# A two-layer flow-matching trunk: the delta rule's block inverse works in place, small products go round four tiles, some loads move forward

## The chip, the cores and the metric

The kernel runs on one core of one Trainium2 chip. Its metric is the device time of one launch in microseconds (us), as the median of several runs. A core has the engines TensorE (PE, its weight loads listed apart as PEld), VectorE (DVE), ScalarE (ACT) and GpSimd (POOL), and SyncE (SP), which here only issues transfers.

## The reference

Two layers of a hybrid trunk for 1024 latent tokens and 128 context tokens, nine tiles of 128 tokens with 1024 channels each. Cut to what matters here:

```python
mod = jax.nn.silu(cond) @ w_mod + b_mod          # 1024 x 3072: shift, scale, gate
h = _rmsnorm(x, g_pre) * (1 + scale) + shift
z = h @ w_in                                     # columns for branches A, B, C
# A: windowed attention with rotary positions   B: gated MLP over 128-token chunks
# C: bidirectional gated DeltaNet, in chunks of 64 tokens:
a_mat = jnp.where(strict, jnp.einsum('bnihd,bnjhd->bnhij', kb, k) * decay, 0.0)
t_mat = lax.linalg.triangular_solve(a_mat + eye, jnp.broadcast_to(eye, a_mat.shape),
                                    left_side=True, lower=True, unit_diagonal=True)
# ... u, w from t_mat; then a scan over the chunks with a 64 x 64 state per head
x = x + gate * _rmsnorm(concat(A, B, C) @ w_out, g_post)
```

The inverse of I + A for each 64 x 64 strictly triangular A is what the title's substitution computes.

## The kernel before

All eight rows of weights are split into a high and a low float16 part, and a projection of one token tile takes 24 matmuls (`proj_tok`, L170). A planner puts the instructions of each engine in an order when the program is built, by a simulated timeline; on the chip each engine then runs its list in that order and waits where data isn't there.

A layer runs two generators side by side (`merge`, L1124). The chain is branch C: gates (`c_gates`, L355), convolution features (`c_features`, L296, matmuls at L312), and `scan` (L419). The fill is `both` (L1187): the MLP, C's gate, attention (`fill`, L1175, called heavy there), and two column groups of the MLP's gate (`b_gate`, L823). Each yields a cost, and `merge` takes fill worth 0.9 of what the chain yields. `b_gate(k)` starts when the chain has put an entry into the list `light`; until then heavy goes on.

In `scan`, head group 0 is prepared, its inverse solved (`lat_solve`, L661) and its 18 scan steps run (`steps`, L549; matmuls L566 to L597, VectorE's copy `vn` at L585), while head group 1 is prepared; then head group 1 is solved and stepped. The context blocks are solved once beside the first preparation. So a layer has three solves, of which two (latent) have 16 blocks per row and one (context) has 4.

A solve is: `diagonals` (L479) gathers the 32 x 32 diagonal blocks, transposes them into a tile M (L497), clears a tile Y (L499) and sets its diagonal to one (L500). `solve` (L503) does the substitution on VectorE, for m from 31 down to 1, with two instructions (L510 multiplies a column of M by a row of Y, L512 subtracts the product from Y). `inverses` (L516) transposes Y two ways (L520), and multiplies for the off-diagonal block: a first run of matmuls of 32 x 32 by 32 x 32 (L527), a copy by ScalarE (L530), negated copies of the diagonal blocks by ScalarE (L537) and GpSimd (L539), a second run (L543). In both runs the outer loop goes over the four (direction, half) sides, which have different rows and columns of the array, and the inner one over the L blocks:

```python
for (r, half, p1, p2) in sides:
    for j in range(L):
        T.matmul(ps[p2:p2 + 32, 32 * j:32 * j + 32], W[p1:p1 + 32, r, j, ...], ...)
```

Each float32 matmul stands in the trace as two PE instructions, so a latent run is 128 of them and a context run 32.

Between the heads of layer 0's attention, `mod` (L210) forms the modulation vectors of layer 1 and the gate of layer 0 from w_mod: a transfer of 512 KB (L245, two blocks of 128 rows, 512 columns, in one of the two staging buffers `st`), then two matmuls per transfer into 32 columns of the array each (L249), round four places j in turn.

Staged weights go through `load_w` (L148): a transfer on ScalarE's queue, ScalarE's high part (L160), VectorE's low part (L161). All other transfers, the transposing ones of attention too (L953, P to PT), go through SP's queue in its order. `out_layer` (L1044) starts per token tile when branch outputs lie in DRAM (`mix_d`); it loads them (OTm, L1054, two buffers) and multiplies by w_out (L1072).

Of the kernel before, what the change touches and what calls it, by code (L numbers as in the profile page):

```python
# [11 lines left out]
F32 = mybir.dt.float32  # L12
# [28 lines left out]
LT = 9  # L41
AHEAD = 6
FILL = 0.9


@with_exitstack
def hybrid_trunk(
# [64 lines left out]
    V.tensor_copy(idb, ident)  # L112
    CK = per.tile([128, 640], F32, name="CK")
    triI = [CK[:, 0:128], CK[:, 128:256]]
    triL = [CK[:, 256:384], CK[:, 384:512]]
    bdones = CK[:, 512:640]
    selc = per.tile([128, 2], F32, name="selc")
# [5 lines left out]
    def masks():  # L123
        dma(CK, cst[:, 0:640])
        ctmp = stg.tile([128, 256], F32, tag="st", name="ctmp")
        dma(ctmp, cst[:, 640:896])
        G.tensor_copy(triIc16, ctmp[:, 0:128].rearrange("p (r c) -> p r c", r=2))
        G.tensor_copy(mneg, ctmp[:, 128:256].rearrange("p (r c) -> p r c", r=2))
        G.tensor_copy(triL16, CK[:, 256:512].rearrange("p (r c) -> p r c", r=2))

# [79 lines left out]
    def mod(l, vt, mp_, csp, AB, wmp=None):  # L210
# [25 lines left out]
        for part in (1, 0, 2):  # L236
            for cb in (2 * part, 2 * part + 1):
                ps = psp()
                for k2 in range(4):
                    if wmp is not None and part < 2:  # L240
                        st = wmp.tile([128, 4, 256], F32, tag="wm", name=nm("wm"), bufs=16)
                    else:
                        st = stg.tile([128, 4, 256], F32, tag="st", name=nm("st"))
                    s = st.rearrange("p a b -> p (a b)").rearrange("p (k c) -> p k c", k=2)
                    dma(s, w_mod[l, 256 * k2:256 * k2 + 256, 512 * cb:512 * cb + 512].rearrange("(k p) c -> p k c", p=128))  # L245
                    for kk in range(2):
                        k = 2 * k2 + kk
                        j = k % 4
                        T.matmul(ps[32 * j:32 * j + 32, :], csp[:, k, :], s[:, kk, :], start=(k < 4), stop=(k >= 4))  # L249
# [105 lines left out]
    def c_gates(l, cp, gp, out):  # L355
        GB = cp.tile([128, 2, 2, 9, 4], F32, name=nm("GB"))
        wab = gp.tile([128, 8, 2, 16], F16, name="wab")
        sab = gp.tile([128, 8, 16], F32, name="sab")
# [60 lines left out]
    def scan(l, cqk, cv_, gates, oacc, ng, NAc, keep, wo, light):  # L419
# [59 lines left out]
        def diagonals(ep, W, L):  # L479
            D = ep[:, 0:64 * L].rearrange("p (n c) -> p n c", c=32)  # L480
            for r in range(2):
                for half in range(2):
                    for a in range(2):
                        rb = 64 * half + 32 * a
                        src = W[rb:rb + 32, r, :, 32 * a:32 * a + 32]
                        dst = D[rb:rb + 32, L * r:L * r + L, :]
                        if half == r:
                            S_.copy(dst, src)
                        else:
                            V.transpose(dst, src)  # L490
            M = ep[:, 1024:2048]
            Dt = D.transpose([0, 2, 1])
            Mt = M.rearrange("p (r c) -> p c r", c=32)
            if L < 16:
                Dt = bc(Dt, 2, 16 // L)
                Mt = Mt.rearrange("p c (x y) -> p c x y", y=2 * L)
# [6 lines left out]
        def solve(ep, M, Y):  # L503
            m3 = M.rearrange("p (r c) -> p r c", c=32)
            y3 = Y.rearrange("p (r c) -> p r c", c=32)
            for m in range(31, 0, -1):
                tmp = ep[:, 3072:3328]
                w = 32 - m
                t3 = tmp[:, 0:m * w].rearrange("p (r c) -> p r c", c=w)
                V.tensor_tensor(t3, m3[:, 0:m, m:m + 1].to_broadcast([128, m, w]),  # L510
                                y3[:, m:m + 1, m:32].to_broadcast([128, m, w]), op=ALU.mult)
                V.tensor_tensor(y3[:, 0:m, m:32], y3[:, 0:m, m:32], t3, op=ALU.subtract)  # L512
                yield 1.0


        def inverses(ep, W, L, Y):  # L516
# [13 lines left out]
            S_.activation(C_[:, 0:32 * L], ps[:, 0:32 * L], AF.Copy, scale=-1.0)  # L530
            for r in range(2):
                for a4 in range(4):
# [8 lines left out]
            for (r, half, p1, p2) in sides:  # L541
                for j in range(L):
                    T.matmul(ps[p1:p1 + 32, 32 * j:32 * j + 32], C_[p2:p2 + 32, 32 * j:32 * j + 32],  # L543
# [117 lines left out]
        def lat_solve(hg, sv):  # L661
            M, Y = diagonals(sv, Ws[hg], 16)
            yield 4.0
            for i, cost in enumerate(solve(sv, M, Y)):
# [7 lines left out]
        with pool(f"gx{l}", 1) as cx, pool(f"gp{l}0", 2) as gp:  # L672
# [3 lines left out]
            for i, _ in enumerate(preps(gp, todo)):  # L676
                if i == 3:
                    M, Y = diagonals(cx, Wc, 4)
                    ctx_solve = solve(cx, M, Y)
                for _ in range(4):  # L680
# [142 lines left out]
    def b_gate(l, bp, k):  # L823

        cs = slice(128 * k, 128 * k + 128)
        w = bp.tile([128, 8, 2, 256], F16, name=nm("wb"), bufs=1)
        load_w((w_in[l, :, C_BU + 128 * k:C_BU + 128 * k + 128], w_in[l, :, C_BG + 128 * k:C_BG + 128 * k + 128]), 256, w)
        sc = IWS * IWS * IWS * 0.5

        def out(ts, th):  # L830
# [46 lines left out]
    def attention(l, other=iter(())):  # L877
        with pool(f"t3{l}", 1, "right") as p1:
# [25 lines left out]
            def prep(p2, kv, t, wq, wa):  # L904
                pq = psp()
                proj_tok(pq[:, 0:256], t, wq)
                proj_tok(pq[:, 256:512], t, wa)
                rt = p2.tile([128, 128], F32, tag="rt", name=nm("rt"))
                dma(rt, rope[t])
                qa = rope_tile(p2, pq[:, 0:256], 4, rt)  # L910
# [93 lines left out]
            for kv in range(2):  # L1004
                with pool(f"t3b{l}{kv}", 2, "right") as p2:
                    if kv == 0:
# [7 lines left out]
                        for t in ordert:  # L1014
                            ps = psp()
                            proj_tok(ps[:, 0:256], t, wkv)
                            rt = p2.tile([128, 128], F32, tag="rt", name=nm("rt"))
                            dma(rt, rope[t])
                            ka = rope_tile(p2, ps[:, 0:128], 2, rt)
# [23 lines left out]

    def out_layer(l, wo, nextAB):  # L1044
# [99 lines left out]
    for l in range(NL):  # L1144
# [14 lines left out]
        cqk = [q.tile([128, 9, 2, 128], F32, name=nm("cqk")) for q in (c0, cp)]  # L1159
        cv_ = [q.tile([128, 9, 128], F32, name=nm("cv")) for q in (c0, cp)]  # L1160
# [26 lines left out]
        def both():  # L1187
            heavy, k = fill(), 0
            while True:
# [5 lines left out]
                elif k < 2:  # L1195
                    with pool(f"bg{l}{k}", 2, "right") as bp:
                        yield from b_gate(l, bp, k)
                    k += 1
# [76 lines left out]
```

## Time and profile before

| what | value |
|---|---|
| median of 3 runs | 1471.59 us (1468.35 to 1475.64) |
| the profiled execution's own time | 1462.98 us |
| its span, first to last instruction | 1460.2 us |
| mean granted TensorE clock | 0.946 |
| PE busy | 1307.0 us (90%) |
| DVE busy | 941.5 us (64%) |
| ACT busy, POOL busy | 616.9 us, 613.4 us (42% each) |

The span is one execution as the hardware profiler saw it; 2.8 us of the execution's time lie outside it. Busy time is a union of the engine's instructions. A matmul's recorded length has a tail that overlaps the next one's start.

### The profile page before, as it was taken

To read this page: it belongs to the slowest core of one execution; us is meant where nothing else is said; L and a number is where in the kernel's file an instruction comes from. 1 tells how busy PE (TensorE), PEld (TensorE's weight loads), DVE (VectorE), ACT (ScalarE), POOL (GpSimd) and SP (SyncE) were. 2 spreads that over 40 slices of the span, in tenths; PEclk is the share of its full clock that TensorE was granted. 3 is DMA by queue.
4 is the path that set the end of the run, shared out by engine and by line. 5 is a ranking of instruction groups with operands and counts; after the bars stand their busy time and mean duration, and the time that the engine had idled before them with its cause. 6 is when DMAs were issued, how large, how long until landed. Compare 5 with 4: busy or idle time off the path is not lost.

```text
span 1460.2 us, 38255 instructions
## 1 busy us (share of the span) xinstructions
PE 1307.0 (90%) x15479; PEld 1009.7 (69%) x15479; DVE 941.5 (64%) x2230; ACT 616.9 (42%) x1411; POOL 613.4 (42%) x818
## 2 busy tenths in 40 slices
PE   6899989899998699959897999999898769987997
PEld 2665567666667587748786655678787658865886
DVE  2865689987646666753446587687875485767333
ACT  2733454434646116732333444332566313665211
POOL 0761245435556135742132432631668403666200
PEclk8999999999999898969998999999999988998999
DMA  9331044839865117673332122242276311877552
GB/s 358 120 80 55 24 113 106 180 105 222 162 171 87 39 32 144 120 221 76 120 131 84 32 63 68 73 95 64 55 142 120 60 49 40 157 115 166 130 181 103
DMA packets 301562, 162.92 MB, mean 112 GB/s; under 512 B 212622, under 2 KB 277938, under 8 KB 301386
## 3 DMA queue, kind: packets, MB, share of 16 engines
q1 hardware_dynamic: 264301, 127.94, 37.4%
q10 hardware_dynamic: 37085, 32.55, 7.6%
q8 instruction: 121, 1.98, 0.6%
q14 instruction: 55, 0.45, 0.1%
HBM read 95.78 MB, written 24.28 MB: 82 GB/s over the span
## 4 chain that ended last, share of the span: by engine, by line
PE 54%; DVE 14%; DMA 13%; issue 7%; POOL 6%; ACT 4%; SPq 1%; ACTq 0%; DVEq 0%; POOLq 0%
PE ps L170 16%; PE ps L1072 12%; PE ps L312 6%; DMA PT<-P 4%; DMA st<-in_w_in_dram 2%; DMA st<-in_w_mod_dram 2%; PE ps L967 2%; POOL P L951 2%; PE ps L249 2%; DVE y L319 1%; DVE sv L512 1%; PE ps L543 1%; PE ps L527 1%; DVE sv L510 1%; DVE wg L161 1%
## 5 line engine op out<-in xcount | busy, mean ns | idle before, releaser
L170 PEld LDWEIGHTS <-X 128*128 128x128 f16 x3888 | 349.6, 100 | 101.2 <-issue 39.3
L170 PE MATMUL ps<-wg,X 128*128 128x256 f16 x2592 | 328.6, 280 | 10.5 <-DVE wg L161 3.9
L951 POOL TENSOR_TENSOR P<-sS,P 128x512 f16<-128x512 f32 (+2 forms) x144 | 150.9, 1053 | 100.9 <-ACT sS L949 100.2
L1072 PEld LDWEIGHTS <-OTm 128*128 128x128 f16 x1728 | 169.1, 99 | 30.5 <-DMA OTm<-mix_d 8.8
L1072 PE MATMUL ps<-wo,OTm 128*128 128x256 f16 x1296 | 152.1, 276 | 7.6 <-DMA OTm<-mix_d 7.6
L312 PE MATMUL ps<-X,wg 128*128 128x512 f16 (+1 forms) x864 | 146.1, 329 | 1.8 <-ACT wg L160 1.4
L946 DVE CUSTOM_DVE_ANT_0 sS<-ps,am,nsk 128x512 f32<-128x512 f32 (+2 forms) x144 | 95.1, 669 | 49.1 <-POOL P L951 24.6
L948 ACT ACTIVATE P<-sS,nmx 128x512 f16<-128x512 f32 (+2 forms) x144 | 94.0, 660 | 73.0 <-DVE nmx L946 67.4
L312 PEld LDWEIGHTS <-wg 128*128 128x128 f16 x864 | 74.0, 99 | 69.1 <-ACT wg L160 1.8
L170 PE MATMUL ps<-wb,X 128*128 128x256 f16 x864 | 102.5, 279 | 14.4 <-ACT wb L160 12.5
L949 ACT ACTIVATE sS<-sS,nmx 128x512 f32<-128x512 f32 (+2 forms) x144 | 95.1, 660 | 4.2 <-DVE OTA L1001 0.4
L145 POOL TENSOR_TENSOR rs<-ms,mhalf 128x1 f32<-128x1 f32 x36 | 20.7, 576 | 171.9 <-DVE ms L1081 103.7
L967 PE MATMUL ps<-Vt,PT 128*128 128x128 f16 (+1 forms) x992 | 67.9, 211 | 22.8 <-DMA PT<-P 21.8
L319 DVE SCALAR_TENSOR_TENSOR y<-zT,cw,y 128x1156 f32<-128x1156 f32 x48 | 68.9, 1439 | 27.4 <-ACT y L317 26.8
L512 DVE TENSOR_TENSOR sv<-sv 128x31 f32<-128x31 f32 (+15 forms) x186 | 78.4, 421 | 4.1
L967 PEld LDWEIGHTS <-PT 128*128 128x128 f16 x992 | 51.1, 100 | 41.6 <-DMA PT<-P 29.7
L510 DVE TENSOR_TENSOR sv<-sv 128x31 f32<-128x31 f32 (+15 forms) x186 | 74.8, 402 | 4.0
L942 PE MATMUL ps<-KT,qT 128*128 128x128 f16 (+2 forms) x272 | 68.6, 269 | 0.0
L288 DVE TENSOR_SCALAR hf<-ps,AB 128x128 f32<-128x128 f32 x117 | 39.7, 402 | 39.3 <-PE ps L281 39.0
L1075 ACT ACTIVATE sq<-ps 128x512 f32<-128x512 f32 x36 | 21.3, 594 | 99.8 <-PE ps L1072 56.8
L941 PE MATMUL ps<-KT,qT 128*128 128x128 f16 (+2 forms) x272 | 60.3, 271 | 3.6 <-DVE nmx L946 1.8
L161 DVE SCALAR_TENSOR_TENSOR wg<-st,wg 128x1024 f16<-128x1024 f32 x44 | 56.0, 1280 | 10.6 <-ACT wg L160 10.4
(265 smaller groups left out, 2723.8 us busy)
## 6 DMA issues: line engine op xcount, KB each, us to landing
st<-in_w_in_dram ACTq DMA_DIRECT2D x38, 512.0 KB
st<-in_w_mod_dram SPq DMA_DIRECT2D x32, 512.0 KB
OTm<-mix_d SPq DMA_DIRECT2D x18, 512.0 KB
wm<-in_w_mod_dram SPq DMA_DIRECT2D x16, 512.0 KB
xt<-in_x_sample_dram SPq DMA_DIRECT2D x16, 512.0 KB
st<-in_w_out_dram ACTq DMA_DIRECT2D x16, 512.0 KB
mix_d<-OTA SPq DMA_DIRECT2D x36, 128.0 KB
xs<-xt SPq DMA_DIRECT2D x9, 512.0 KB
```

The source lines that it names most:

```text
L161: V.scalar_tensor_tensor(dst[:, 4 * h:4 * h + 4, 1, :cols], s, WS, hi, op0=ALU.mult, op1=ALU.subtract)
L170: T.matmul(ps, X[:, t, k, a, :], wg[:, k, b, c0:c0 + n], start=(i == 0), stop=(i == 23))
L312: T.matmul(ps[:, 0:n], wg[:, k, b, 128 * hg:128 * hg + 128], X[:, t0:t1, k, a, :], start=(i == 0), stop=(i == 23))
L319: V.scalar_tensor_tensor(y, zT[:, tap:tap + 1156], cw[:, tap * 6 + ct:tap * 6 + ct + 1], y, op0=ALU.mult, op1=ALU.add)
L510: V.tensor_tensor(t3, m3[:, 0:m, m:m + 1].to_broadcast([128, m, w]), y3[:, m:m + 1, m:32].to_broadcast([128, m, w]), op=ALU.mult)
L512: V.tensor_tensor(y3[:, 0:m, m:32], y3[:, 0:m, m:32], t3, op=ALU.subtract)
L946: V.tensor_tensor_reduce(sS[:, 0:nk], ps[:, 0:nk], mk, -0.125, nsk[:, hh:hh + 1], ALU.add, ALU.min, accum_out=nmx[:, h:h + 1])
L948: S_.activation(P16[:, 0:nk], sS[:, 0:nk], AF.Exp, bias=nmx[:, h:h + 1], scale=-1.0)
L949: S_.activation(sS[:, 0:nk], sS[:, 0:nk], AF.Exp, bias=nmx[:, h:h + 1], scale=-1.0, accum_out=sm[:, h:h + 1])
L951: G.tensor_tensor(P16[:, nk:2 * nk], sS[:, 0:nk], P16[:, 0:nk], op=ALU.subtract)
L967: T.matmul(pops[:, 128 * h:128 * h + n], PT[:, a * nb + j, :], Vt[:, blist[j], kv].rearrange("p s d -> p (s d)")[:, 0:n], start=(i == 0), ...
L1072: T.matmul(ps[:, 256 * i:256 * i + 256], OTm[:, k, a, :], w[:, k, b, :], start=(n == 0), stop=(n == 23))
```

## The change

Cut to its core:

```diff
-            M = ep[:, 1024:2048]
+            Y = ep[:, 2048:3072]
...
-            V.transpose(Mt, Dt)
-            Y = ep[:, 2048:3072]
-            V.memset(Y, 0.0)
-            V.memset(Y[:, 0:1024:33], 1.0)
-            return M, Y
+            V.transpose(Yt, Dt)
+            V.memset(Y[:, 0:1024:33], -1.0)
+            return Y
...
-            for m in range(31, 0, -1):
+            for m in range(30, 0, -1):
...
-                w = 32 - m
+                w = 31 - m
-                V.tensor_tensor(t3, m3[:, 0:m, m:m + 1].to_broadcast([128, m, w]),
-                                y3[:, m:m + 1, m:32].to_broadcast([128, m, w]), op=ALU.mult)
-                V.tensor_tensor(y3[:, 0:m, m:32], y3[:, 0:m, m:32], t3, op=ALU.subtract)
-                yield 1.0
+                V.tensor_tensor(t3, y3[:, 0:m, m:m + 1].to_broadcast([128, m, w]),
+                                y3[:, m:m + 1, m + 1:32].to_broadcast([128, m, w]), op=ALU.mult)
+                V.tensor_tensor(y3[:, 0:m, m + 1:32], y3[:, 0:m, m + 1:32], t3, op=ALU.subtract)
+                yield 31 / 30
...   in inverses, both runs:
-            for (r, half, p1, p2) in sides:
-                for j in range(L):
+            for j in range(L):
+                for (r, half, p1, p2) in sides:
...   and its copies lose their factor of -1:
-                        S_.activation(dst, src, AF.Copy, scale=-1.0)
+                        S_.copy(dst, src)
-                        G.tensor_scalar(dst, src, -1.0, None, op0=ALU.mult)
+                        G.tensor_copy(dst, src)
...   in mod, for the transfers through the staging buffers:
+                    ch, kq = k2 // 2, k2 % 2
+                    c0 = 512 * cb + 256 * ch
+                    dma(st, w_mod[l, 512 * kq:512 * kq + 512, c0:c0 + 256].rearrange("(k p) c -> p k c", p=128))
+                    for j in range(4):
+                        T.matmul(ps[32 * j:32 * j + 32, 256 * ch:256 * ch + 256], csp[:, 4 * kq + j, :], st[:, j, :],
+                                 start=(kq == 0), stop=(kq == 1))
...   in lat_solve: the entry in light for head group 1 right after diagonals
+            if hg:
+                light.append(hg)
             yield 4.0
...
-                if i == (2 if hg else LT):
+                if not hg and i == LT:
...   in both, EARLY = (8.0, 1.0); b_gate yields 0.0 once, right after its load_w
+                        gate = b_gate(l, bp, k)
+                        yield next(gate)
+                        n = 0.0
+                        while n < EARLY[k]:
+                            got = next(heavy, None)
+                            if got is None:
+                                break
+                            n += got
+                            yield got
+                        yield from gate
...   in b_gate one transfer per pair of tiles:
-            for j, t in enumerate(ts):
-                dma(mix_d[t, :, 4 + k].rearrange("p s c -> p (s c)"), ot[:, j].rearrange("p s c -> p (s c)"))
+            dma(mix_d[ts[0]:ts[0] + n, :, 4 + k].rearrange("t p s c -> p t (s c)"), ot[:, 0:n].rearrange("p t s c -> p t (s c)"))
...   in attention the rotary table once per layer, in place of a tile (rt) per use:
+            rts = p1.tile([128, 9, 128], F32, name="rts")
+            dma(rts, rope.rearrange("t p c -> p t c"))
...   the masks CK are loaded in c_gates once per layer, as its first transfer:
+        CK = gp.tile([128, 640], F32, name="CK")
+        dma(CK, cst[:, 0:640])
...   out_layer's two OTm buffers are halves of one tile in the pool of cqk[0]:
+            OT2 = c0.tile([128, 2, 8, 2, 128], F16, tag="cq0", name=nm("OT2"))
-                OTm = p1.tile([128, 8, 2, 128], F16, tag="OTm", name=nm("OTm"), bufs=2)
+                OTm = OT2[:, ti % 2]
...
+        out_layer(l, wo, c0, nxt[1])
         rs.close()
-        out_layer(l, wo, nxt[1])
```

M and Y become one tile: the substitution overwrites the transposed blocks, with -1 on the diagonal, and yields the negated inverse.

## Rows read from the trace of the kernel before

**Rows 1.** Busy time by stage: engine busy (instructions), PE clock, DMA share, GB/s.

```profile
373.00:500.00 127.00, 111.36 (x1816) 86.89 (x1817) 75.65 (x209) 62.08 (x162) 68.00 (x105) 0.97 0.54 116
500.00:550.00 50.00, 45.10 (x547) 38.92 (x547) 34.58 (x88) 11.02 (x22) 13.44 (x19) 0.84 0.20 54
550.00:653.00 103.00, 82.89 (x1276) 67.21 (x1274) 69.44 (x175) 59.52 (x142) 61.96 (x86) 0.86 0.73 162
```

**Rows 2.** Chain that ended last, in time: start us, us, what.

```profile
360.24 3.86 PE ps L527 x128
...
534.62 3.86 PE ps L527 x128
538.48 4.61 PE ps L170 x26
...
650.02 3.55 DMA OTm<-mix_d
```

**Rows 3.** Timeline, the small products: start us, us, engine, line, count [idle before].

```profile
294.80 0.89 PE L527 MATMUL ps<-sv,NAc 32*32 32x32 f32 x32
...
360.17 3.93 PE L527 MATMUL ps<-sv,NA 32*32 32x32 f32 x128
...
599.79 0.45 PE L566 MATMUL ps<-ident,qk 64*64 64x64 f32 x8
...
1049.49 5.47 PE L527 MATMUL ps<-sv,NA 32*32 32x32 f32 x128 [1.33 <-DVE sv L520]
```

**Rows 4.** Line L539 on POOL: duration ns min/median/max, first and last start.

```profile
L539 POOL TENSOR_SCALAR NA<-sv x16: 1477/1481/1484, 355.7 to 1218.1; 32x512 f32<-32x512 f32 x16
```

**Rows 5.** Timeline of PE, the modulation's matmuls.

```profile
240.65 1.06 PE L249 MATMUL ps<-st,csp 128*32 128x512 f32 x8
...
246.56 1.05 PE L249 MATMUL ps<-st,csp 128*32 128x512 f32 x4
...
408.01 1.05 PE L249 MATMUL ps<-st,csp 128*32 128x512 f32 x4 [1.86 <-DMA st<-in_w_mod_dram]
```

**Rows 6.** Groups by line: busy us, mean ns | idle before and what ended it.

```profile
L249 PE MATMUL ps<-st,csp 128*32 128x512 f32 x128 | 31.4, 619 | 8.8 <-DMA st<-in_w_mod_dram 8.8
L566 PE MATMUL ps<-ident,qk 64*64 64x64 f32 x576 | 36.3, 238 | 4.2 <-ACT qw L572 1.3 <-DVE NA L463 1.3 <-DVE of L751 0.9
L512 DVE TENSOR_TENSOR sv<-sv 128x31 f32<-128x31 f32 (+15 forms) x186 | 78.4, 421 | 4.1
L499 DVE MEMSET sv<- 128x1024 f32 x6 | 5.5, 912 | 1.4 <-DVE sv L490 1.1 <-issue 0.2 <-DVE xc L802 0.2
L869 DVE TENSOR_TENSOR ra<-ps,rt 128x256 f32<-128x256 f32 (+1 forms) x54 | 20.1, 372 | 34.9 <-PE ps L170 22.8 <-DMA rt<-in_rope_dram 5.5 <-DMA out_dram<-ra 1.8
```

**Rows 7.** Timeline around head group 1's solve in layer 0, and its counterpart in layer 1.

```profile
496.00 0.91 DVE L499 MEMSET sv<- 128x1024 f32 x1 [0.28 <-DVE sv L490]
496.83 0.23 DVE L585 COPY vn<-ps 128x128 f32<-128x128 f32 x1
...
497.20 0.69 PE L593 MATMUL ps<-vn,kd 64*64 64x64 f32 x8 [3.27 <-DVE vn L585]
...
500.39 1.38 SPq L647 DMA_DIRECT2D out_dram<-S  x2
503.33 2.00 ACT L160 ACTIVATE wb<-st 128x1024 f16<-128x1024 f32 x2 [8.51 <-DVE sv L512]
504.44 0.80 PE L170 MATMUL ps<-wb,X 128*128 128x256 f16 x3 [5.66 <-ACT wb L160]
...
1184.92 2.00 ACT L160 ACTIVATE wb<-st 128x1024 f16<-128x1024 f32 x2 [8.58 <-DMA out_dram<-S]
```

**Rows 8.** Timeline at the start of layer 1.

```profile
771.15 0.38 SPq L359 DMA_DIRECT2D sab<-in_w_in_dram  x1
...
787.52 2.06 PE L170 MATMUL ps<-wab,X 128*128 128x16 f16 x70
...
790.71 2.13 POOL L291 TENSOR_TENSOR X<-hf,X 128x1024 f16<-128x1024 f32 x1 [0.41 <-ACT X L290]
```

More of the change, by code (lines that the diff above doesn't have):

```diff
@@ L42 @@
 AHEAD = 6
+EARLY = (8.0, 1.0)
 FILL = 0.9
@@ L112, in hybrid_trunk @@
     V.tensor_copy(idb, ident)
[L113 to L116, printed above, removed]
     selc = per.tile([128, 2], F32, name="selc")
@@ L123, in masks @@
     def masks():
-        dma(CK, cst[:, 0:640])
-        ctmp = stg.tile([128, 256], F32, tag="st", name="ctmp")
-        dma(ctmp, cst[:, 640:896])
+        ctmp = stg.tile([128, 512], F32, tag="st", name="ctmp")
+        dma(ctmp[:, 0:256], cst[:, 640:896])
+        dma(ctmp[:, 256:512], cst[:, 256:512])
         G.tensor_copy(triIc16, ctmp[:, 0:128].rearrange("p (r c) -> p r c", r=2))
         G.tensor_copy(mneg, ctmp[:, 128:256].rearrange("p (r c) -> p r c", r=2))
-        G.tensor_copy(triL16, CK[:, 256:512].rearrange("p (r c) -> p r c", r=2))
+        G.tensor_copy(triL16, ctmp[:, 256:512].rearrange("p (r c) -> p r c", r=2))
     mhalf = per.tile([128, 18], F32, name="mhalf")
@@ L241, in mod @@
                         st = wmp.tile([128, 4, 256], F32, tag="wm", name=nm("wm"), bufs=16)
[L242 to L249, printed above, removed]
+                        s = st.rearrange("p a b -> p (a b)").rearrange("p (k c) -> p k c", k=2)
+                        dma(s, w_mod[l, 256 * k2:256 * k2 + 256, 512 * cb:512 * cb + 512].rearrange("(k p) c -> p k c", p=128))
+                        for kk in range(2):
+                            k = 2 * k2 + kk
+                            j = k % 4
+                            T.matmul(ps[32 * j:32 * j + 32, :], csp[:, k, :], s[:, kk, :], start=(k < 4), stop=(k >= 4))
+                        continue
+                    ch, kq = k2 // 2, k2 % 2
+                    c0 = 512 * cb + 256 * ch
+                    st = stg.tile([128, 4, 256], F32, tag="st", name=nm("st"))
+                    dma(st, w_mod[l, 512 * kq:512 * kq + 512, c0:c0 + 256].rearrange("(k p) c -> p k c", p=128))
+                    for j in range(4):
+                        T.matmul(ps[32 * j:32 * j + 32, 256 * ch:256 * ch + 256], csp[:, 4 * kq + j, :], st[:, j, :],
+                                 start=(kq == 0), stop=(kq == 1))
                 mp = mp_.tile([128, 512], F32, tag="mp", name=nm("mp"), bufs=2 if PIPE else 1)
@@ L356, in c_gates @@
         GB = cp.tile([128, 2, 2, 9, 4], F32, name=nm("GB"))
+        CK = gp.tile([128, 640], F32, name="CK")
+        dma(CK, cst[:, 0:640])
+        triI = [CK[:, 0:128], CK[:, 128:256]]
+        triL = [CK[:, 256:384], CK[:, 384:512]]
+        bdones = CK[:, 512:640]
         wab = gp.tile([128, 8, 2, 16], F16, name="wab")
@@ L529, in inverses @@
             C_ = ep[:, 3328:3840]
-            S_.activation(C_[:, 0:32 * L], ps[:, 0:32 * L], AF.Copy, scale=-1.0)
+            S_.copy(C_[:, 0:32 * L], ps[:, 0:32 * L])
             for r in range(2):
@@ L536, in inverses @@
                     if a4 % 2:
-                        S_.activation(dst, src, AF.Copy, scale=-1.0)
+                        S_.copy(dst, src)
                     else:
-                        G.tensor_scalar(dst, src, -1.0, None, op0=ALU.mult)
+                        G.tensor_copy(dst, src)
             ps = psw()
-            for (r, half, p1, p2) in sides:
-                for j in range(L):
+            for j in range(L):
+                for (r, half, p1, p2) in sides:
                     T.matmul(ps[p1:p1 + 32, 32 * j:32 * j + 32], C_[p2:p2 + 32, 32 * j:32 * j + 32],
@@ L661, in lat_solve @@
         def lat_solve(hg, sv):
-            M, Y = diagonals(sv, Ws[hg], 16)
+            Y = diagonals(sv, Ws[hg], 16)
+            if hg:
+                light.append(hg)
             yield 4.0
-            for i, cost in enumerate(solve(sv, M, Y)):
-                if i == (2 if hg else LT):
+            for i, cost in enumerate(solve(sv, Y)):
+                if not hg and i == LT:
                     light.append(hg)
@@ L677, in scan @@
                 if i == 3:
-                    M, Y = diagonals(cx, Wc, 4)
-                    ctx_solve = solve(cx, M, Y)
+                    Y = diagonals(cx, Wc, 4)
+                    ctx_solve = solve(cx, Y)
                 for _ in range(4):
@@ L827, in b_gate @@
         load_w((w_in[l, :, C_BU + 128 * k:C_BU + 128 * k + 128], w_in[l, :, C_BG + 128 * k:C_BG + 128 * k + 128]), 256, w)
+        yield 0.0
         sc = IWS * IWS * IWS * 0.5
@@ L907, in prep @@
                 proj_tok(pq[:, 256:512], t, wa)
-                rt = p2.tile([128, 128], F32, tag="rt", name=nm("rt"))
-                dma(rt, rope[t])
+                rt = rts[:, t, :]
                 qa = rope_tile(p2, pq[:, 0:256], 4, rt)
@@ L1016, in attention @@
                             proj_tok(ps[:, 0:256], t, wkv)
-                            rt = p2.tile([128, 128], F32, tag="rt", name=nm("rt"))
-                            dma(rt, rope[t])
+                            rt = rts[:, t, :]
                             ka = rope_tile(p2, ps[:, 0:128], 2, rt)
@@ L1042, in attention, with out_layer @@
                     finish(p2, *prev.pop())
-    def out_layer(l, wo, nextAB):
+    def out_layer(l, wo, c0, nextAB):
         last = l == NL - 1
@@ L1158, in hybrid_trunk @@
         c0 = rs.enter_context(pool(f"c0{l}", 1, "right"))
-        cqk = [q.tile([128, 9, 2, 128], F32, name=nm("cqk")) for q in (c0, cp)]
+        cqk = [q.tile([128, 9, 2, 128], F32, tag=f"cq{i}", name=nm("cqk")) for i, q in enumerate((c0, cp))]
         cv_ = [q.tile([128, 9, 128], F32, name=nm("cv")) for q in (c0, cp)]
```

8 lines of the change are left out of this document (3 added, 5 removed).

## The prediction, made before the result was known

> **What bounds the kernel now.** I read the page first: PE is busy 90% of the span, DVE 64%. An average hides stages, so the table of stretches came next [rows 1]. In the 127 us of layer 0's first scan PE works 111.4 us and every other engine under 76; in the solve of head group 1 (500 to 550) PE has 45.1 of 50 at a granted clock of 0.84; in the second scan (550 to 653) PE has 82.9 of 103, with DMA at 0.73, the highest share of the three. So a microsecond taken from PE's list counts nearly whole in the first two and perhaps half in the third. The chain of waits then says what stands on the path: among its pieces are all eight runs of small products of the latent solves, as whole blocks of 3.9 us and more, of which two stand in the rows [rows 2]. Last I read the timeline around those blocks, the modulation's matmuls, the two solves of head group 1 and the layer boundary [rows 3 to 8].
>
> **The small products of the inverse.** A latent run is 128 instructions in 3.93 us [rows 3]. An instruction's own recorded length is longer than the distance to the next one's start (0.24 us for L566 [rows 6]); with some 0.2 us for the last one's, one starts every 29 ns. Consecutive ones use the same rows and columns of the array, and none can start before the last has streamed. With the loops exchanged, four neighbours use four different row groups and four different column groups. Does the array overlap them? Two rows bear on it. Eight matmuls of twice the columns that alternate between two corners of the array take 0.45 us [rows 3], 0.21 without the last one's own length [rows 6], where eight starts on one place at twice 29 ns would take 0.46. And eight modulation matmuls on four column groups take 1.06 us where four on two groups take 1.05 [rows 5]: four places cost what two cost. I take full overlap of four: 32 rounds of 29 ns and that length, about 1.2 us, so 2.7 us less per latent run. There are two runs in each of four latent solves: 8 x 2.7 = 21.6 us. A context run of 32 takes 0.89 us [rows 3] and becomes 0.45; four of them give 1.8. One latent run goes at half clock (5.47 us [rows 3]) and would give more; I leave that out. Sum: -23.5 us, bounds 0 (no overlap) and -25.
>
> The Trainium skill, "TensorEngine Tiling (Array Packing)", section "Restrictions and Gotchas", says that different row tiles cannot access the same PSUM bank at once; here all four write one bank, and by that rule the term would be 0. The 0.45 us row has two row tiles in one bank too and speaks against it, for two places; no row has four.
>
> What can eat this gain: between the two runs GpSimd copies four blocks, 1.48 us each [rows 4], 6 us after the first transpose. In layer 0's second solve PE fills the gap with 4.61 us of projection [rows 2]; with the first run 2.7 us shorter, filler still covers the copies' end. If the planner puts the filler elsewhere, the copies set the second run and the first run's gain is lost (below). The copies as such I cost at nothing: the same elements, by a copy in place of a multiply.
>
> **The modulation's loads.** 32 transfers feed 128 instructions. In the timeline they stand as 29 groups: 26 of four (first and last shown) and three of eight, where two transfers had both landed [rows 5]. A group of four is two passes one behind the other, 1.05 us; one instruction is recorded at 0.62 [rows 6], so a pass is 0.43. With half the columns and four places, each transfer's eight instructions are two passes of 0.22, and 0.43 us less per group that stood alone: 26 x 0.43 = 11.2 us of PE. The groups of eight gain nothing. But PE already waited 8.8 us for these transfers [rows 6], once 1.86 at 408 [rows 5], and where the landing decides, a faster matmul waits longer. A transfer's rows shrink from 2 KB to 1 KB, as w_in's have them; I see no cost in that. I take -8, bounds -2 (nothing but the time between a matmul and the next issue) and -11.
>
> **The substitution.** L512 takes 78.4 us over six solves [rows 6], and L510, its partner of the same sizes and count, I put at as much: 26 us a solve. The new one has 30 pairs for 31 and 4960 elements a pair-sum for 5456: between 0.8 (by count) and 2.4 us (by elements) less; I take 1.5. The clear of Y goes, 0.91 us a time [rows 6]. That is 14 us of DVE over six solves. Most of it is covered: beside context and first latent solve PE is full of attention, and in head group 1's solve, projections of the gate run about as long as the substitution. On the path I count the clear where it stood ahead of the scan's copy `vn`, while PE waited 3.27 us for it [rows 7]: 0.9 in each layer; and 1 us per layer for the shorter solve of head group 1, whose end the first run awaits. Sum: -4, bounds 0 and -14.
>
> **The gate's weights and the fill around them.** In both layers ScalarE stands 8.5 us before it converts the gate's weights, and PE stands 5.66 us behind it in layer 0 [rows 7]. The wait is not for the weights: the row of layer 1 names the store of the final state, and in layer 0 that store is issued 2.9 us before the conversion starts [rows 7]: `wb` lies in memory that the scan's tiles held. The earlier load does not move that store. The heads put between load and gate (at least 1.0 of cost, two heads) can start their scores in the hole, but their exponentials are in ScalarE's list around the same blocked conversion: -1 us per layer. The entry in `light` one yield of 4.0 and two steps earlier puts some units of heavy behind gate 1 instead of ahead of it; they move from one PE-full stretch to another and I cost them at nothing. If they left more of the first scan without fill (PE is idle 15.6 of its 127 us already [rows 1]), each unit would cost about its microsecond, up to 5 per layer. Sum: -2, bounds +10 and -11 (both holes closed).
>
> **The transfers.** 54 loads of `rt` become two of 576 KB. DVE waited 5.5 us for them [rows 6]; they also leave SP's queue, in which the transposes of P stand, as do 16 stores of the gate's outputs. First use of the table needs all of it landed, hidden behind the key projections' weights. I take -2, bounds 0 and -6. The masks' 320 KB now go ahead of `sab` in SP's queue in layer 1, whose first conversion waits from 771.15 to 773.46 for that load [rows 8]: one issue of 0.38 us and a share of the bandwidth, +1, bounds +0.4 and +2.5. OTm's new place changes no wait that I can see: the first OTm transfer follows the store it depends on in the chain and takes 3.55 us [rows 2], wherever it lands. `out_layer`'s other pools sit 5.6 KB deeper, over attention's tiles; their loads have some 25 us until use. Costed at 0, 2 at most.
>
> **The sum.** -23.5 - 8 - 4 - 2 - 2 + 1 = -38.5 us against the profiled execution's 1462.98: 1424.5. The median of the runs shown is 8.6 above that execution; the same distance gives 1433, 2.6% less. What a measurement of this kernel can tell from no change is about 0.5%, 7.4 us (1464.2 to 1479.0).
>
> **Rivals.**
> First, half comes back: GpSimd's copies set the second run (2.7 us lost in each of four latent solves, 10.8), and the landing of the modulation's transfers takes the 6 us between -8 and -2. -22, so 1450. For it: the copies' 6 us against 1.2 + filler [rows 2, 4] and the 1.86 us wait [rows 5]. Against: filler stood in all four gaps.
> Second, the small products stay serial, because four rows of tiles into one bank are not four columns into one: the change then doesn't do what its first part says. -38.5 + 23.5 = -15, so 1457. For it: no row shows four row groups. Against: the 0.45 us row [rows 3].
> The rule of "TensorEngine Tiling (Array Packing)" above is this rival.
> Third, slower: OTm's two buffers are now halves of one tile. If waits go by the tile and not by the half, each load waits for the matmuls of the tile before, and each of 16 later tiles pays a load of 3.55 us [rows 2]: +57, with the rest +18, so 1490. It decides from 2.4 us a tile on. Against it: X is one tile as well, and PE reads parts of it at 787.52 while GpSimd writes another part at 790.71 [rows 8].
>
> **How the numbers follow.** The forecast's case, gains mostly whole, 0.63, by its own bounds 1418 to 1446; the first rival 0.22, the second 0.09, the third 0.06. The range is 1412 to 1460: from the forecast with closed holes or full modulation gain, up to the second rival with a few microseconds on it; outside are the third rival, a quarter of the second and the edges of the first two cases, under 2 in 10. Faster by over 0.5% is the first case, the first rival and nearly all of the second: 0.92. Within: 0.03. Slower: the third rival, 0.05.
>
> **What would show it.** Right: L527 and L543 stand as runs of 128 in 1.1 to 1.4 us; each L249 group of eight in 0.6 us; L499 is gone, L510 and L512 have 180 instructions each; ScalarE still waits for the state's store before `wb`; OTm loads run ahead of their tile. Wrong: small products at 3.9 us a run (second rival); a gap on PE just before L543 that GpSimd ends (first); gaps of over 2 us before each tile's L1072 (third). The prediction also fails if the planner's order, made anew for every instruction, opens holes in the scans that none of the steps above names.

## The result and the profile after

The changed kernel takes 1436.9 us (median of 4 runs, 1431.5 to 1439.2), the kernel before 1473.6 us beside it: ratio 0.9723 (95% interval 0.9688 to 0.9757). In later runs of both it was 0.9757 (0.9722 to 0.9792), 1437.3 against 1476.6 us. The mean of the two ratios is 0.974, some 38 us less. 1433 was forecast, so the size is right; the terms behind it are so only in part.

The profiled execution of the changed kernel took 1439.21 us, with a span of 1436.3 us. First its stages, cut where those of [rows 1] now lie (columns as there):

```profile
361.00:488.00 127.00, 111.57 (x1852) 88.50 (x1849) 68.44 (x193) 60.08 (x158) 65.69 (x103) 0.97 0.56 117
488.00:536.00 48.00, 39.90 (x572) 33.48 (x572) 37.39 (x90) 11.54 (x21) 9.15 (x17) 0.86 0.17 50
536.00:634.00 98.00, 80.34 (x1262) 65.29 (x1262) 67.51 (x179) 59.07 (x147) 62.99 (x85) 0.92 0.73 156
```

The first scan looks as before; in the solve PE works 39.9 us where it worked 45.1, and in the second scan the clock is 0.92 where it was 0.86. Now the small products, which answer to [rows 3], from the timeline of PE (first run L532, second run L548):

```profile
296.00 0.45 PE L532 MATMUL ps<-sv,NAc 32*32 32x32 f32 x32
345.30 1.42 PE L532 MATMUL ps<-sv,NA 32*32 32x32 f32 x128
350.58 0.24 PE L548 MATMUL ps<-NA,sv 32*32 32x32 f32 x2
355.43 0.24 PE L548 MATMUL ps<-NA,sv 32*32 32x32 f32 x2
357.80 1.40 PE L548 MATMUL ps<-NA,sv 32*32 32x32 f32 x124
...
1021.65 1.93 PE L532 MATMUL ps<-sv,NA 32*32 32x32 f32 x128 [3.57 <-DVE sv L525]
...
1201.46 1.29 PE L548 MATMUL ps<-NA,sv 32*32 32x32 f32 x128
```

128 instructions stand in 1.3 to 1.4 us where they took 3.93, and 32 in 0.45 where they took 0.89. The first run at 1021.65 took 1.93 us, behind an idle time of 3.57; 1.2 GHz was granted there (the mean clock is 0.82 from 1022 to 1047, below). The second run of the solve that starts at 345 is split: PE starts two instructions at 350.58, two at 355.43, and between them does filler (other work that was ready). Groups by line, as [rows 6] and [rows 4] (busy us, mean ns | idle before and what ended it):

```profile
L251 PE MATMUL ps<-st,csp 128*32 128x256 f32 x256 | 24.1, 390 | 10.3 <-DMA st<-in_w_mod_dram 10.0
L548 PE MATMUL ps<-NA,sv 32*32 32x32 f32 x512 | 6.9, 194 | 0.0
L532 PE MATMUL ps<-sv,NA 32*32 32x32 f32 x512 | 6.3, 204 | 3.6 <-DVE sv L525 3.6
L517 DVE TENSOR_TENSOR sv<-sv 128x30 f32<-128x30 f32 (+9 forms) x180 | 70.5, 392 | 4.4
L876 DVE TENSOR_TENSOR ra<-ps,rts 128x256 f32<-128x256 f32 (+1 forms) x54 | 20.1, 373 | 25.6 <-PE ps L167 16.7 <-POOL ql L925 3.6 <-DMA rts<-in_rope_dram 2.6
L544 POOL COPY NA<-sv 32x512 f32<-32x512 f32 x16 | 9.7, 604 | 11.7 <-DVE sv L525 11.2
L1080 PE MATMUL ps<-wo,OT 128*128 128x256 f16 x1296 | 150.9, 275 | 3.3 <-DMA OT<-mix_d 3.3
```

And the hole at the gate of [rows 7], from the timeline:

```profile
489.25 0.69 PE L598 MATMUL ps<-vn,kd 64*64 64x64 f32 x8 [2.36 <-DVE vn L590]
...
492.40 1.38 SPq L652 DMA_DIRECT2D out_dram<-S  x2
495.26 2.00 ACT L157 ACTIVATE wb<-st 128x1024 f16<-128x1024 f32 x2 [7.39 <-DVE sv L517]
496.37 0.80 PE L167 MATMUL ps<-wb,X 128*128 128x256 f16 x3 [5.54 <-ACT wb L157]
```

It is as wide as before: 5.54 us against 5.66, and the conversion starts 2.9 us after the state's store, as before.

**Where the time went.** A second execution of each kernel was profiled (below). PE's busy time was split in the trace by the level that its clock was granted. As an estimate, a microsecond at 1.2 GHz is counted as half a microsecond of work at 2.4 GHz, so "work at 2.4 GHz" is busy time less half of that part.

| us | before | before, again | after | after, again |
|---|---|---|---|---|
| execution | 1462.98 | 1476.41 | 1439.21 | 1434.24 |
| PE busy | 1307.0 | 1311.3 | 1272.2 | 1272.1 |
| of it at 1.2 GHz | 115.4 | 122.0 | 99.9 | 98.3 |
| work at 2.4 GHz | 1249.3 | 1250.3 | 1222.3 | 1222.9 |
| PE idle in the span | 153.2 | 163.3 | 164.1 | 160.2 |

Between the means of the two pairs the profiled time falls by 33.0 us: 27.2 less work, 9.8 less time lost at the lower clock, 3.9 more idle. Between two executions of a kernel the work repeats within 1 us, the other two within some 10; between kernels with the same matmuls in another order the work too differs, by up to 7 us (1220.9 in `e12_best`, 1228.0 in `e11_poolmul`). The first profile of the kernel before was a quick one: 11 us under the median of its runs above.

### The profile page after: what moved, and what is told of

Read it like the earlier page. It is cut to its first block, busy times and chain, and to the rows that moved or that the text cites. A ratio compares the mean times of both kernels' runs of the same rounds, so it can differ in the third digit from the quotient of the medians.

```text
span 1436.3 us, 38355 instructions
## 1 busy us (share of the span) xinstructions
PE 1272.2 (89%) x15607; PEld 985.7 (69%) x15607; DVE 922.8 (64%) x2212; ACT 613.0 (43%) x1411; POOL 591.1 (41%) x818
## 5 line engine op out<-in xcount | busy, mean ns | idle before, releaser
L167 PE MATMUL ps<-wg,X 128*128 128x256 f16 x2592 | 324.1, 277 | 17.7 <-ACT wg L157 4.5
L1080 PEld LDWEIGHTS <-OT 128*128 128x128 f16 x1728 | 169.6, 99 | 25.2 <-DMA OT<-mix_d 3.7
L1080 PE MATMUL ps<-wo,OT 128*128 128x256 f16 x1296 | 150.9, 275 | 3.3 <-DMA OT<-mix_d 3.3
L975 PEld LDWEIGHTS <-PT 128*128 128x128 f16 x992 | 49.6, 99 | 45.1 <-DMA PT<-P 35.4
L517 DVE TENSOR_TENSOR sv<-sv 128x30 f32<-128x30 f32 (+9 forms) x180 | 70.5, 392 | 4.4
L515 DVE TENSOR_TENSOR sv<-sv 128x30 f32<-128x30 f32 (+9 forms) x180 | 68.9, 383 | 3.9
L157 ACT ACTIVATE wg<-st 128x1024 f16<-128x1024 f32 x44 | 45.3, 1054 | 44.8 <-DMA st<-in_w_in_dram 28.0
```

Of the source, the lines that this page charges most:

```text
L167: T.matmul(ps, X[:, t, k, a, :], wg[:, k, b, c0:c0 + n], start=(i == 0), stop=(i == 23))
L515: V.tensor_tensor(t3, y3[:, 0:m, m:m + 1].to_broadcast([128, m, w]), y3[:, m:m + 1, m + 1:32].to_broadcast([128, m, w]), op=ALU.mult)
L517: V.tensor_tensor(y3[:, 0:m, m + 1:32], y3[:, 0:m, m + 1:32], t3, op=ALU.subtract)
L975: T.matmul(pops[:, 128 * h:128 * h + n], PT[:, a * nb + j, :], Vt[:, blist[j], kv].rearrange("p s d -> p (s d)")[:, 0:n], start=(i == 0), ...
L1080: T.matmul(ps[:, 256 * i:256 * i + 256], OTm[:, k, a, :], w[:, k, b, :], start=(n == 0), stop=(n == 23))
```

## The experiments

All ratios are to the kernel before on the same chip, with 95% intervals; us are against its median there.

**The parts alone, in the kernel before.** The loop order:

```diff
-            for (r, half, p1, p2) in sides:
-                for j in range(L):
+            for j in range(L):
+                for (r, half, p1, p2) in sides:
```

> The kernel before with one edit: the two loops of the small products exchanged, nothing else. Theory A (each part is worth its TensorE time): eight latent runs go from 3.93 to 1.3 us and four context runs from 0.89 to 0.45, so about 22 us less than the kernel before. Theory B (the copies set the second run): GpSimd still multiplies, 1.48 us a block, four blocks one behind the other, so the second run of each latent solve starts as late as before and half comes back: 11 us less, with TensorE waiting ahead of the second run for GpSimd. Theory C (the order of the instructions, made anew, matters as much as the parts): anything from 0 to 30 us less, with the difference in places that hold no small products.

0.9875 (0.9829 to 0.9921), 18 us less (12 to 25). That is theory A's size; B's 11 lies just outside the interval. Undoing it in the changed kernel (`e4_noloop`, the same lines the other way):

> The changed kernel with the two loops of the small products put back, nothing else undone. Theory A: 22 us more than the changed kernel, so 15 us less than the kernel before. Theory C (part of the small products' gain was already lost in the changed kernel, to filler that stands between the two runs and to idle time in layer 1): 8 to 15 us more than the changed kernel.

0.9898 (0.9868 to 0.9928): against the changed kernel's 0.974 the loops are worth some 23 us there (some 18 to 29 with both intervals). Theory A, not C.

What comes behind these runs shows in the windows of 25 us from each first run's start, with the columns of [rows 1] and a sum. They are of the kernel before (second profile; then one row of its first), the changed kernel without the loops, the changed kernel, its second profile (the sum alone), and the kernel before with the loops alone (`e1_loop`, the sum alone):

```profile
361.00:386.00 25.00, 25.00 (x412) 18.07 (x411) 9.55 (x24) 8.83 (x19) 6.95 (x8) 0.86 0.58 130
540.00:565.00 25.00, 25.00 (x420) 21.44 (x418) 14.07 (x28) 13.45 (x27) 15.01 (x19) 0.93 0.44 105
1056.00:1081.00 25.00, 25.00 (x390) 21.18 (x389) 11.73 (x32) 11.33 (x25) 10.86 (x11) 0.73 0.31 57
1239.00:1264.00 25.00, 25.00 (x409) 21.55 (x408) 13.31 (x36) 13.32 (x33) 9.78 (x19) 0.93 0.46 116
sum 100.00, PE 100.00 PEld 82.23 DVE 48.67 ACT 46.93 POOL 42.60; mean PE 25.00 PEld 20.56 DVE 12.17 ACT 11.73 POOL 10.65
```

```profile
360.00:385.00 25.00, 25.00 (x452) 18.77 (x451) 9.38 (x27) 11.68 (x29) 11.66 (x13) 1.00 0.68 144
```

```profile
531.00:556.00 25.00, 25.00 (x352) 20.29 (x350) 8.56 (x20) 8.22 (x15) 7.53 (x14) 0.73 0.24 65
...
sum 100.00, PE 99.60 PEld 82.25 DVE 41.63 ACT 49.41 POOL 34.59; mean PE 24.90 PEld 20.56 DVE 10.41 ACT 12.35 POOL 8.65
```

```profile
345.00:370.00 25.00, 24.27 (x504) 17.53 (x502) 14.60 (x41) 15.90 (x38) 11.46 (x14) 1.00 1.04 229
524.00:549.00 25.00, 23.81 (x475) 19.57 (x473) 16.66 (x37) 13.87 (x28) 12.43 (x20) 1.00 0.50 123
1022.00:1047.00 25.00, 23.00 (x455) 18.47 (x446) 14.26 (x38) 14.91 (x37) 10.84 (x14) 0.82 0.45 71
1197.00:1222.00 25.00, 21.26 (x417) 17.06 (x417) 15.70 (x44) 16.21 (x41) 12.62 (x21) 0.93 0.65 128
sum 100.00, PE 92.34 PEld 72.62 DVE 61.23 ACT 60.88 POOL 47.34; mean PE 23.08 PEld 18.15 DVE 15.31 ACT 15.22 POOL 11.84
```

```profile
sum 100.00, PE 90.16 PEld 69.98 DVE 59.46 ACT 59.93 POOL 44.87; mean PE 22.54 PEld 17.50 DVE 14.86 ACT 14.98 POOL 11.22
```

```profile
sum 100.00, PE 92.55 PEld 71.41 DVE 63.07 ACT 61.55 POOL 56.89; mean PE 23.14 PEld 17.85 DVE 15.77 ACT 15.39 POOL 14.22
```

With the old loops PE has a backlog behind the runs and is idle for half a microsecond of the 100 at most; with the new ones it is idle for 7 to 10 us of the 100, waiting for engines that do more in the same time (DVE 61 us for 49). So about a third of what the loops free is handed to waits. But the clock is lower behind most of the old runs, with PE recorded as busy throughout. In the first profile of the kernel before, the two runs of layer 0's second latent solve start at 534.55 and 543.02 and last 3.9 and 5.2 us; 1.2 GHz was granted from 539.0 to 542.4 and from 545.8 to 552.7. Behind the runs at 360 of the same profile the clock did not fall (1.00, the row by itself). From each first run's start to 12 us behind the second run's end, the four latent solves hold 17 to 38 us at 1.2 GHz in all seven executions with the old loops (this study's two of the kernel before, the four parts without loops, `e4_noloop`), and 3 to 12 us in all seven with the new (27 in both profiles of the kernel before, 10 with the loops alone; 9 and 12 after, 30 without the loops). The means are 28 and 8 us; 20 us less at half speed are some 10 us of time. That gives the waits back. Over the whole span PE is busy at 1.2 GHz for 115 to 148 us in the seven with the old loops and for 89 to 113 in the seven with the new.

The modulation's loads alone:

```diff
-                    dma(s, w_mod[l, 256 * k2:256 * k2 + 256, 512 * cb:512 * cb + 512].rearrange("(k p) c -> p k c", p=128))
+                    dma(st, w_mod[l, 512 * kq:512 * kq + 512, c0:c0 + 256].rearrange("(k p) c -> p k c", p=128))
+                    for j in range(4):
+                        T.matmul(ps[32 * j:32 * j + 32, 256 * ch:256 * ch + 256], csp[:, 4 * kq + j, :], st[:, j, :],
```

> The kernel before with the modulation's new loads and matmuls alone. Theory A: TensorE's matmuls of this line come down by 7 to 11 us and the time by about 8 us. Theory B (the landing of the transfers decides): matmuls shorter by as much, but the wait for st grows from 8.8 us to about 15 us, and the time comes down by 2 us or less.

0.9965 (0.9938 to 0.9992), 5 us less (1 to 9). Theory A's 8 is inside, B's 2 too. The group of matmuls is 24.6 us busy in place of 31.4, and here the wait for `st` did not grow (6.3 us for 8.8). In the whole change it is 10.3 us (10.5 in the second profile, against 8.8 and 9.7 before).

The substitution alone:

```diff
-            Y = ep[:, 2048:3072]
-            V.memset(Y, 0.0)
-            V.memset(Y[:, 0:1024:33], 1.0)
+            V.memset(Y[:, 0:1024:33], -1.0)
...
-            for m in range(31, 0, -1):
+            for m in range(30, 0, -1):
...
-                        G.tensor_scalar(dst, src, -1.0, None, op0=ALU.mult)
+                        G.tensor_copy(dst, src)
```

> The kernel before with the negated substitution in place alone (GpSimd's and ScalarE's copies without their factor too). Theory A: VectorE loses 14 to 19 us of work, of which 4 us were on the path: 4 us less. Theory B (all of it covered): no difference that can be told, 0 to 2 us. Both expect GpSimd's copies at 0.60 us in place of 1.48 us, as in the changed kernel.

0.9924 (0.9892 to 0.9955), 11 us less (7 to 16): more than either. PE's work is the same within 2 us (1248.3); it is idle time that went, and much of it far from any solve. The output stage's matmuls by line, before again and with the substitution alone:

```profile
L1072 PE MATMUL ps<-wo,OTm 128*128 128x256 f16 x1296 | 154.3, 279 | 7.6 <-DMA OTm<-mix_d 7.6
```

```profile
L1069 PE MATMUL ps<-wo,OTm 128*128 128x256 f16 x1296 | 151.5, 276 | 0.4 <-DMA OTm<-mix_d 0.4
```

7.2 us of waits for OTm are gone, with the same loads in the same two buffers: the planner, given a shorter solve, put output tiles elsewhere. Why there was not traced further. The profiled execution of this run was the fastest of its 12 (1453.83 us against a median of 1463.41), so the profile shows more idle time gone than the median does.

The gate's weights alone:

```diff
+            if hg:
+                light.append(hg)
...
-                        yield from b_gate(l, bp, k)
+                        gate = b_gate(l, bp, k)
+                        yield next(gate)
...
+                        while n < EARLY[k]:
+                            got = next(heavy, None)
...
+                        yield from gate
```

> The kernel before with the gate weights' early load alone: the entry in the list light right after diagonals, and heads of attention worth 8.0 and 1.0 of cost between the load and its conversion. Theory A: the conversion still waits for the store of the final state, 1 us less per layer from scores that stand in the hole, 2 us less in all. Theory B: the first scan loses fill and TensorE idles longer in it: 5 to 10 us more.

1.0043 (1.0019 to 1.0067), 6 us more (3 to 10): theory B's size, but not its mechanism. Layer 0's first scan, from the end of the latent solve to the last `vn`, before again and with the early load alone:

```profile
372.00:502.00 130.00, 113.88 (x1811) 86.08 (x1809) 74.78 (x208) 64.61 (x167) 67.59 (x105) 0.97 0.52 114
```

```profile
368.00:508.00 140.00, 124.14 (x1923) 95.16 (x1920) 77.61 (x213) 68.44 (x178) 73.22 (x110) 0.96 0.60 128
```

PE is idle 16.1 us of the one and 15.9 of the other; in layer 1's first scan 19.4 and 19.8. Undone in the changed kernel:

> The changed kernel without the gate weights' early load and without the heads ahead of their conversion. Theory A: 2 us more than the changed kernel. Theory B (in layer 1 the last scan gave time back because fill had been used up earlier): up to 5 us less than the changed kernel.

0.9741 (0.9711 to 0.9771), no difference from 0.974. So it costs by itself, and in company no cost can be told from none. The profile with the early load alone has more idle time than before again in the last scan of layer 1 and behind it. From the windows of that stage (some 10 us before head group 1's first run to the last `vn`), before again, with the early load alone, after, the changed kernel without it, and the changed kernel without the loops, which has the early load too:

```profile
1231.00:1383.00 152.00, 137.50 (x2082) 112.75 (x2081) 90.83 (x261) 83.43 (x210) 91.66 (x128) 0.93 0.64 129
```

```profile
1227.00:1390.00 163.00, 144.27 (x2159) 118.20 (x2157) 92.18 (x267) 83.95 (x212) 92.42 (x128) 0.95 0.65 130
```

```profile
1186.00:1342.00 156.00, 131.74 (x2105) 106.81 (x2102) 90.16 (x262) 83.37 (x209) 87.20 (x126) 0.95 0.63 125
```

```profile
1189.00:1337.00 148.00, 128.12 (x2086) 104.17 (x2084) 89.37 (x260) 83.26 (x208) 86.79 (x125) 0.97 0.65 128
```

```profile
1217.00:1368.00 151.00, 138.35 (x2105) 113.22 (x2103) 88.74 (x264) 83.53 (x211) 88.85 (x127) 0.94 0.65 132
```

PE is idle 14.5, 18.7, 24.3, 19.9 and 12.7 us of it. The idle time there doesn't follow the part: the stage holds more PE work with the early load alone than before (144.3 us, 137.5), and the kernel without the loops has the early load and the least idle time. Why the part costs 6 us by itself stays open.

The transfers alone (rotary table and masks once per layer, one store per pair, OTm in the earlier pool):

```diff
+            rts = p1.tile([128, 9, 128], F32, name="rts")
+            dma(rts, rope.rearrange("t p c -> p t c"))
...
+        CK = gp.tile([128, 640], F32, name="CK")
+        dma(CK, cst[:, 0:640])
...
+            OT2 = c0.tile([128, 2, 8, 2, 128], F16, tag="cq0", name=nm("OT2"))
```

> The kernel before with the transfers alone: rotary table once per layer, masks once per layer, one store per pair of tiles, OTm in the earlier pool. Theory A: the waits for rt fall from 5.5 to under 3 us, OTm loads run ahead of their tile and the waits for them come down by 8 us over both layers, but most of this is DVE's or covered: 1 to 2 us less. Theory B (the loads for the output stage end the waits there): 5 to 10 us less, the difference standing in the last 130 us of each layer.

1.0003 (0.9983 to 1.0024): no difference. OT waits fell from 7.6 to 5.6 us, DVE's for the table from 5.5 to 1.9. Neither theory's gain is there; A's 1 to 2 us can't be told from none.

**The copies.** The changed kernel with GpSimd's old kind of instruction:

```diff
-                        G.tensor_copy(dst, src)
+                        G.tensor_scalar(dst, src, 1.0, None, op0=ALU.mult)
```

> The changed kernel with GpSimd's copies of the diagonal blocks as a multiply by 1.0 in place of a copy. Theory A (the copies stand in the shadow of the first run and of the filler): they take 1.48 us each again, the second run starts where it did, time within 3 us of the changed kernel. Rival (the prediction's first rival): the second run of each latent solve waits for GpSimd, up to 2.7 us in each of four solves, 5 to 11 us more.

0.9713 (0.9684 to 0.9742), no slower than 0.974. From its timeline, the first latent solve:

```profile
345.47 6.17 POOL L544 TENSOR_SCALAR NA<-sv 32x512 f32<-32x512 f32 x4
...
347.74 1.44 PE L532 MATMUL ps<-sv,NA 32*32 32x32 f32 x128
350.39 0.56 ACT L535 COPY sv<-ps 128x512 f32<-128x512 f32 x1
353.00 0.24 PE L548 MATMUL ps<-NA,sv 32*32 32x32 f32 x2
```

The copies take 1.48 us each again and end at 351.64; the second run starts 5.26 us after the first, in the changed kernel 5.28 (345.30 to 350.58). Filler and ScalarE's copy cover them: PE's matmuls of the second runs (L548) stand idle for nothing, 0.0 us, in this run as in the changed kernel. The copies' half of the first rival is refuted, at either price of a copy.

**The hole at the gate.** The scan's state tiles get a pool of their own (`Sp`, opened before `gp` and `gs`), so that `wb` no longer lies where the last state is being stored from:

```diff
-                Sn = sp.tile([128, 2, 64], F32, tag="S", name=nm("S"), bufs=4)
+                Sn = Sp.tile([128, 2, 64], F32, tag="S", name=nm("S"), bufs=4)
```

> The changed kernel with the scan's state tiles in a pool of their own, so that the weights of the gate no longer wait for the store of the final state before ScalarE converts them. Theory A (that store holds the conversion): ScalarE starts it about 3 us earlier in each layer, TensorE's wait of 5.54 us behind it falls to about 2.5 us, and the time by 3 to 6 us. Rival (another release comes just behind the store, or the filler that covers the hole is missed later): TensorE's wait stays over 4.5 us, or moves, and the time stays within 2 us.

```profile
490.29 2.00 ACT L157 ACTIVATE wb<-st 128x1024 f16<-128x1024 f32 x2 [1.91 <-issue]
491.40 0.80 PE L167 MATMUL ps<-wb,X 128*128 128x256 f16 x3 [0.71 <-ACT wb L157]
492.95 1.37 SPq L652 DMA_DIRECT2D out_dram<-S  x2
494.08 1.22 DVE L158 SCALAR_TENSOR_TENSOR wb<-st,wb 128x1024 f16<-128x1024 f32 x1
495.35 2.93 PE L167 MATMUL ps<-wb,X 128*128 128x256 f16 x13 [3.15 <-DVE wb L158]
```

The conversion now runs ahead of the store: the store had held it. But what was late next was VectorE's low part, which its list holds behind the first instructions of the substitution, and PE waits 3.15 us for that. 0.9707 (0.9674 to 0.9741). With the load ahead of `diagonals` as well:

```diff
+            if hg:
+                light.append(hg)
+                yield 1.5
             Y = diagonals(sv, Ws[hg], 16)
```

> The changed kernel with the scan's state tiles in a pool of their own, and the gate weights of head group 1 loaded ahead of the gathering of the diagonal blocks. In the run with the pool alone TensorE still waited 0.71 + 3.15 us for the weights, the second of these for VectorE's low part, which stood behind the first instructions of the substitution. Theory A: with the earlier load the low part comes ahead of the substitution, TensorE's wait falls under 1.5 us in each layer, and the time is 4 to 8 us below the changed kernel. Rival: the substitution starts as much later, and the time stays within 2 us of the run with the pool alone.

0.9711 (0.9683 to 0.974): PE's wait for the low part is 2.91 us, the rival's case. Both versions lie 4 to 5 us under the changed kernel, a difference that these intervals do not tell from none; the kernel with the slower copies lies as low.

**The same kernels again.**

> The kernel before once more, unchanged, for a second profile. Theory A (the first profile was a fast one of its kind, its execution at 1462.98 us against a median of 1474): the second execution takes 1470 to 1480 us, and what it has more is TensorE's time at the half clock and idle time, 10 us or so together, with the same work at full clock. Rival (the profile adds or takes nothing and the changed kernel's own profile was a slow one): 1460 to 1466 us again.

1476.41 us: theory A. It spends 6.6 us more at 1.2 GHz (3.3 us of time) and is idle 10.1 us more than in its first profile, at the same work.

> The changed kernel once more, unchanged, for a second profile and more times. Both theories of the size: 0.9723 of the kernel before within 0.003; TensorE's time at the half clock differs from the first profile's 99.9 us by up to 20 us, its work at full clock by under 2 us.

0.9757, 0.0034 above the first and just past the expected 0.003; work at 2.4 GHz within 0.6 us, at 1.2 GHz 98.3 us.

## Why the prediction was right, and where it was not

**Small products, -23.5.** Right in mechanism: four places overlap. By line these runs fell from 39.0 us (18.0 and 17.4 for the latent ones, 3.6 for the context) to 15.0. Of the 24 us, 3 are clock, as the old runs stand at 1.2 GHz for 8.8 of their 39 us and the new for 2.2; counted at 2.4 GHz, as in the table above, the fall is 21. The second rival doesn't hold here: four row groups, each with a column group of its own, write one bank, 128 instructions in 1.3 to 1.4 us. The rule of the Trainium skill, "TensorEngine Tiling (Array Packing)", section "Restrictions and Gotchas", that different row tiles cannot access the same PSUM bank at once, was quoted for that rival, and these runs speak against it. The step left out the one run at half clock ("I leave that out") and had no term for the clock behind the runs: with both, some 10 us around them, as much as in the whole span. It also took PE's freed time as gained whole, where 7 to 10 us of it became waits in the 100 us from the runs on. The two misses are nearly of a size and of opposite sign, which is luck.

**Modulation, -8.** Right in mechanism: between the first profiles -7.3 us of matmuls (of 11.2 worked out), a wait 1.5 us longer, groups of eight at 0.64 us. Alone it measures 5 us (1 to 9).

**Substitution, -4.** VectorE's two instructions of the substitution take 139.4 us where they took 153.2 (L510 took 74.8 of them, not L512's 78.4), 2.3 us less a solve, near the upper of the two prices. PE's wait for `vn` in layer 0 fell by 0.91 us (3.27 to 2.36), as worked out. The 1 us per layer for head group 1 was wrong: from the start of the scan's last `vn` to the end of that substitution it is 2.2 us shorter in layer 0 (33.2 to 31.0) and 1.1 in layer 1 (32.6 to 31.5), but PE's idle time up to the first run stays at 6.5 us in both, so what left the stage is filler that runs elsewhere. The 11 us that the part gives alone are for the larger part idle time elsewhere, which no step named.

**Early weights, -2.** The hole stayed, as said, and for the reason said (`e8_spool`). The gain at its edge did not show. Alone the part costs 6 us, within the bound of +10. That bound was kept for fill missing in the first scan, and there the profile shows none missing; the cause stays open.

**Transfers and masks, -1.** None measured. OTm's loads run ahead (waits 3.3 us), so the third rival is refuted. The masks ahead of `sab` cost ScalarE what was worked out: from the first of the two issues (747.36) to its conversion (750.91) pass 3.55 us where 2.31 passed before, and ScalarE waits 2.94 us there for 1.03.

**The sum.** -38.5 was forecast against the profiled execution, and some 38 were measured between medians, but by other terms: work -27, not -31.5; the clock -10, not 0; idle time +4, not the -7 that the other parts were to bring. These three add up to -33, the difference between the profiled executions; the other 5 us lie within their scatter. So the mechanism of the two largest terms was right, and the total is so close partly by luck, because the misses cancel. The parts measured alone add up to -28 (uncertain by some 10), so a gain in company of 10 us can't be told from none. What stays open: which entries of the planner's order decide the idle time, which moves by 5 to 10 us in stages that a part doesn't touch.

## What to carry to other kernels

Where four independent small matmuls have four places in the array, write the loop so that neighbours use different ones; here the cost of the old order was not only its own length but the clock around and behind it. When a part of a full engine's list is taken away, read the stretch just behind: the backlog that hid the other engines' latencies shrinks with it. A planner's order moves idle time by as much as a small edit is worth, so price such an edit with several executions and a split into work, clock and idle time, not with one profile.

## What was not expected of the hardware

GpSimd takes 0.604 us for a copy of 32 x 512 float32 and 1.481 us for the same tile through a multiply by a constant (L544 in the changed kernel and in `e11_poolmul`). And PE's clock was granted at 0.73 to 0.93 in stretches in which PE is recorded as busy for 25.00 of 25 us: among what it did before the fall were runs of 32 x 32 products on one place at a time. With four places at a time 1.00 was granted in the changed kernel's stretch at the same solve of layer 0 (524 to 549). It is not so at every solve: 1.00 stands behind one pair of old runs (360 to 385), and 0.82 at a new one (1022 to 1047), where PE had stood idle for 3.57 us.
